# Adding seven sums of squares on VectorE, starting the turns of queries and keys earlier, and reordering the attention's first loads in a one-core layer kernel

## The chip, the core and the metric

The kernel runs on one core of a Trainium2 chip. The metric is device time in microseconds. The kernel before takes 584.43 us, the median of 3 runs (584.33 to 585.26).

## What is computed

One layer of a streaming encoder, in fp32, on 1024 tokens of width 1024 with 16 learned meta tokens in front. All three mixers read the same normalised input through one projection, and their outputs share one output projection:

```python
u = rms_norm(h, ln_w)                                # h: meta tokens + x, 1040 x 1024
cx, cb, cc, cz, cq, ckv, krope, mz, rq, rk, rv, rz = split(u @ w_in)
y_conv = cb * (causal_conv3(cc * cx) + conv_b) * silu(cz)               # width 256
q = rms_norm(rms_norm(cq) @ w_uq)                    # 8 heads of 64 + 32 rotary
k_nope, v = split(rms_norm(ckv) @ w_ukv); k = rms_norm([k_nope, krope])
y_mla = softmax(mask(rope(q) @ rope(k).T)) @ v * silu(mz)               # width 512
y_ret = retention(rope(rq), rope(rk), rv) * silu(rz)                    # width 256
out = (h + concat(y_conv, y_mla, y_ret) @ w_out)[16:]
```

The mask is causal by chunks of 64 tokens. The input norm is a factor per token, r = (mean(h*h) + eps)^-0.5, so the kernel multiplies un-normalised x with the weights and applies r afterwards.

## The kernel before

**Products in parts.** Every fp32 operand of a large product is split in a high part, a cast to the 4-byte matmul type by ScalarE, and a low part, the rest, by VectorE (`split`, L102 to L109). `mm3` (L111) then issues three matmuls, high x high, high x low and low x high, all recorded under L114. Weights come through `load_w` (L117): load, high part on ScalarE (L105), low part (L106) on VectorE, or on GpSimd where k % 3 == 2.

**Order.** The program is written in a loop order, and a scheduler orders each engine's instructions from that by its own estimate of durations. Buffers come from pools; where a tile is used again its next writer waits for the last reader. Loads go through the queue of SP, the gate weights' first ones through ScalarE's.

**Start (L190 to L235).** x^T comes in eight slices of 128 rows by 1040 columns (`xs`). Each is scaled by the norm's weight and split in four tiles: `xah`, `xal` (528 columns: meta tokens and the first 512) and `xbh`, `xbl` (the other 512). The casts are L108 on ScalarE, the low parts L109 on VectorE. ScalarE squares the slice (`xsq`, L224), and GpSimd adds the squares into `con` (L225; the first slice's squares go straight into it). The weights of the attention's gate, `wmz`, are split slice by slice. TensorE adds the slice's share to five PSUM banks of the gate `mz`, fifteen matmuls a slice.

**Norms (L242 to L255).** Nine small matmuls of `con` with ones give the sums of squares per token (`ssp`). VectorE scales them (`vx`), GpSimd takes the reciprocal root (`r`, L100), VectorE builds diagonal tiles of it (`dg`, L252), and a matmul of these with ones gives r as a row on every partition (`rps`, L254). While this runs, TensorE computes the rest of the gate. In the same stretch the up-projection weights come through one staging tile `ust` and are split (`uq`, `uk`).

**Latents, retention, convolution.** Then follow the latent projection with the attention's queries and keys, which go to memory token by token (`q_s`, `k_s`); the retention's projection and its recurrence; and the convolution in two halves of channels, each in three steps `conv_cx`, `conv_cz`, `conv_cb`. `feat` (L607) computes one projection of the convolution into one of two PSUM banks; `ccs` is the product of two of them.

**Turns (L549 to L592).** The attention wants queries and keys with features on the partitions. Eight turns, one for the keys or queries of two heads, do this in four parts: load (0), 32x32 block transposes on VectorE (1, L564), splits (2), stores to `T_s` (3). `turns()` is called once per projection step, and `slot` counts the calls: 0 to 15 in the retention, then one per convolution step, and from 36 on one per step of the attention. `BEGIN` holds the slot at which each turn starts; its parts follow 2, 3 and 4 slots later.

**Attention and output.** `load_head` brings one head's keys and queries, `load_pair` the values of two heads. `score` computes scores `S` and their exponentials on ScalarE (`pr`, L762), GpSimd normalises (L771), TensorE transposes (`pTp`, L784), ScalarE copies (`pt`, L790), and the products with the values (`o`, L825) follow. The outputs of convolution and retention (`y_s`) are multiplied with their rows of `w_out` in the gaps, token tile by token tile: `y_split` (L837) loads `ysrc` and casts it (`yh`, `yl`), `load_wo` brings the weights (`wos`), `partial` computes. The attention's own rows of `w_out` come last.

Of the kernel before, what the change touches and what calls it, by code (L numbers as in the profile page):

```python
# [7 lines left out]
F32 = mybir.dt.float32  # L8
F32R = mybir.dt.float32r
# [41 lines left out]
def trunk(tc, ins, outs):  # L51
# [121 lines left out]
    with tc.tile_pool(name="ps0", bufs=1, space=PSUM, reuse_waits="tile") as ps0:  # L173
# [18 lines left out]
        for k in range(KT):  # L192
# [27 lines left out]
            if k == 0:  # L220
                nc.scalar.activation(con[:, :L], st, AF.Square)
            else:
                sq = hp_pool.tile([P, L], F32, tag="v", name=f"xsq{k}")
                nc.scalar.activation(sq, st, AF.Square)  # L224
                nc.gpsimd.tensor_tensor(con[:, :L], con[:, :L], sq, op=ALU.add)  # L225
            if k:
# [322 lines left out]
    turned, slot = {}, [0]  # L549
    BEGIN = (3, 6, 10, 17, 21, 25, 29, 36)  # L550

    def turn(i, part):
# [14 lines left out]
        elif part == 2:  # L567
            dst = turned[i][0]
            for j in range(2):
                hi = hp_pool.tile([P, 3, 256], F32R, tag="v" if i < 6 else "k", name=f"th{i}_{j}")  # L570
                x = dst[:, 3 * j:3 * j + 3]
                if which:
                    split(hi, x.bitcast(F32R), x)
                else:

                    for c in range(3):
                        split(hi[:, c], x[:, c].bitcast(F32R), x[:, c], scale=wqk[:, c:c + 1] if c < 2 else None)
                turned[i].append(hi)
        else:
            dst, *hi = turned.pop(i)  # L580
            for j in range(2):
                nc.sync.dma_start(T_s[which][hp, 0, :, 3 * j:3 * j + 3], hi[j].bitcast(F32))
            nc.sync.dma_start(T_s[which][hp, 1], dst)
# [31 lines left out]
    def load_head(h):  # L615
        for which in (1, 0):
            for x, src in zip((qT, kT)[which][h % 2], T_s[which][h // 2]):
                src = src.rearrange("(i f) c r -> c f i r", i=4)
                o = NM * which
                for c in range(3):  # L620
                    nc.sync.dma_start(x[32 * c:32 * c + 32, o:o + SEQ].bitcast(F32).rearrange("p (i r) -> p i r", i=4), src[3 * (h % 2) + c])
        for i, m_ in enumerate((kmh, kml)):
            nc.gpsimd.tensor_copy(kT[h % 2][i][:96, :NM], m_[:, h].bitcast(F32))

# [85 lines left out]
    ps1, close_ps1 = pool("ps1", space=PSUM)  # L710
    kT = [[kp_.tile([104, LP], F32R, name=f"kt{i}{s}") for s in "hl"] for i in range(2)]
    qT = [[kp_.tile([104, SEQ], F32R, name=f"qt{i}{s}") for s in "hl"] for i in range(2)]
    msk = at1.tile([P, LP], F32, tag="pr", name="msk")
# [3 lines left out]
    for i in range(2):  # L717
        nc.vector.tensor_copy(qT[i][0][96:104], msk[96:104, :SEQ])
        nc.vector.tensor_copy(kT[i][0][96:104], msk2[96:104])
        for j in range(2):  # L720
            nc.gpsimd.memset(kT[i][j][:96, L:].bitcast(mybir.dt.uint32), 0)
        nc.gpsimd.memset(qT[i][1][96:104].bitcast(mybir.dt.uint32), 0)
        nc.gpsimd.memset(kT[i][1][96:104].bitcast(mybir.dt.uint32), 0)
    late = {}
# [13 lines left out]
    if True:  # L738
        prs, pts = {}, {}

        def score(h, t):
# [6 lines left out]
            for i in range(0, nb, 2):  # L748
                n = min(2, nb - i)
                sp = pst("s", f"S{h}_{t}_{i}").rearrange("p (b c) -> p b c", b=2)  # L750
                for j in range(n):
                    mm3(sp[:, j, :w], [q[:, ts_] for q in qT[h % 2]], [k[:, (i + j) * w:(i + j) * w + w] for k in kT[h % 2]], True, True)
                at["dve"] = nc.vector.tensor_reduce(sm[:, i // 2:i // 2 + 1], sp[:, :n, :w], axis=AX.XY, op=ALU.max, negate=True).ins  # L753
                chunks.append((sp[:, :n, :w], i * w, (i + n) * w, n))
# [82 lines left out]
        def y_split(t):  # L837
            src = wsp.tile([P, 512], F32, tag="ws", name=f"ysrc{t}")
            nc.sync.dma_start(src.rearrange("p (k q) -> p k q", k=4), y_s.rearrange("k p q -> p k q")[:, :, t * P:t * P + P])
            ysp[t] = [at1.tile([P, 4, P], F32R, tag=f"y{c}", name=f"y{c}{t}", bufs=2) for c in "hl"]  # L840
            split(ysp[t][0], ysp[t][1], src.rearrange("p (k q) -> p k q", k=4), lo_eng=nc.gpsimd)
# [15 lines left out]
    cuts = [load_wo(k, 0) for k in (0, 1, 6, 7)]  # L857
    for h in range(2):
        load_head(h)
    conv_cx(1, 1, 1)  # L860
# [5 lines left out]
    while cuts:  # L866
        cuts.pop(0)()
    y_split(0)
    conv_cb(1, 1)
# [6 lines left out]
    ym = [ymp.tile([P, SEQ], F32, name=f"ym{i}") for i in range(4)]  # L876
    for i in range(4):
        nc.sync.dma_start(ym[i], mz_s[i])
    late["at2"], close_at2 = pool("at2", LA - 2)
# [10 lines left out]
    for n in range(len(seq) + 1):  # L890
        if n + LA < len(seq):
            score(*seq[n + LA])
        if n < len(seq):
# [10 lines left out]
        if n < len(seq):  # L904
# [145 lines left out]
```

## Time and profile before

| | |
|---|---|
| Median of 3 runs | 584.43 us |
| The profiled execution's own time | 585.46 us |
| Its span, first to last instruction | 583.6 us |
| TensorE (PE) busy | 566.4 us, 97% |
| VectorE (DVE) busy | 353.6 us, 61% |
| ScalarE (ACT) busy | 255.0 us, 44% |
| GpSimd (POOL) busy | 235.4 us, 40% |
| Mean granted TensorE clock | 0.993 |

The span is taken on the core from the first to the last instruction; the execution's time is 1.86 us longer. "Busy" leaves out branches, semaphores and the issuing of loads. The granted clock is a share of full speed: 1.00 is 2.4 GHz, 0.50 is 1.2 GHz. A wait is the idle time of an engine just before an instruction, put down to the instruction that released it last. In names, `<-` stands between what an instruction writes and what it reads, and a DMA share over 1 means that more transfers were open than there are engines.

### The profile page before, as it was taken

To read this page: it belongs to the slowest core of one execution; us is meant where nothing else is said; L and a number is where in the kernel's file an instruction comes from. 1 tells how busy PE (TensorE), PEld (TensorE's weight loads), DVE (VectorE), ACT (ScalarE), POOL (GpSimd) and SP (SyncE) were. 2 spreads that over 40 slices of the span, in tenths; PEclk is the share of its full clock that TensorE was granted. 3 is DMA by queue.
4 is the path that set the end of the run, shared out by engine and by line. 5 is a ranking of instruction groups with operands and counts; after the bars stand their busy time and mean duration, and the time that the engine had idled before them with its cause. 6 is when DMAs were issued, how large, how long until landed. Compare 5 with 4: busy or idle time off the path is not lost.

```text
span 583.6 us, 9535 instructions
## 1 busy us (share of the span) xinstructions
PE 566.4 (97%) x3294; PEld 473.7 (81%) x3294; DVE 353.6 (61%) x769; ACT 255.0 (44%) x598; POOL 235.4 (40%) x327
## 2 busy tenths in 40 slices
PE   9959999999999999999999998899999999999997
PEld 5747889998888888888889877688888888887886
DVE  5974848887736661686445655856756756655032
ACT  7732455576334441543122226645545544654000
POOL 4842246867502321162321637524434534454000
PEclk9979999999999999999999999999999999999999
DMA  8535504357303641446157798937536538113086
GB/s 310 174 87 172 185 21 147 144 199 229 114 0 95 223 137 53 108 164 217 55 179 234 210 253 297 303 117 179 149 114 172 146 98 228 37 54 128 0 290 232
DMA packets 61952, 91.29 MB, mean 156 GB/s; under 512 B 5808, under 2 KB 36144, under 8 KB 61776
## 3 DMA queue, kind: packets, MB, share of 16 engines
q1 hardware_dynamic: 58304, 84.39, 47.0%
q10 hardware_dynamic: 3600, 6.29, 2.9%
q8 instruction: 26, 0.43, 0.3%
q14 instruction: 22, 0.18, 0.1%
HBM read 57.07 MB, written 33.59 MB: 155 GB/s over the span
## 4 chain that ended last, share of the span: by engine, by line
PE 84%; DVE 3%; DMA 2%; POOL 1%; ACT 1%; issue 1%; SPq 0%; DVEq 0%; ACTq 0%; POOLq 0%
PE r L114 16%; PE S L114 8%; PE out L114 8%; PE part L114 7%; PE A L114 7%; PE o L825 6%; PE cv L114 6%; PE pTp L784 5%; PE mz L114 4%; PE cz L114 3%; PE qps L114 3%; PE cb L114 3%; PE kps L114 1%; PE vps L114 1%; PE rsp L502 1%; PE rop L519 1%
## 5 line engine op out<-in xcount | busy, mean ns | idle before, releaser
L762 ACT ACTIVATE pr<-S,smx 128x144 f32<-128x144 f32 (+8 forms) x72 | 50.3, 700 | 36.4 <-DVE smx L753 25.6
L753 DVE TENSOR_REDUCE smx<-S 128x1 f32<-128x144 f32 (+8 forms) x72 | 50.7, 705 | 23.6 <-PE S L114 13.3
L770 POOL TENSOR_SCALAR pm<-pr,smx 128x16 f32<-128x16 f32 x64 | 18.4, 288 | 85.5 <-DVE smx L768 77.6
L784 PE MATMUL pTp<-ident,pr 128*128 128x128 f32 x288 | 46.0, 277 | 2.4 <-POOL pr L771 1.7
L790 ACT COPY pt<-pTp 128x512 f32<-128x512 f32 (+2 forms) x64 | 32.1, 504 | 36.7 <-PE pTp L784 36.6
L771 POOL TENSOR_SCALAR pr<-pr,smx 128x128 f32<-128x128 f32 (+3 forms) x64 | 48.0, 750 | 0.0
L784 PEld LDWEIGHTS pTp<-ident,pr 128*128 128x128 f32 x288 | 34.2, 140 | 11.4 <-issue 2.8
L476 POOL TENSOR_SCALAR kw<-qk,con 128x64 f32<-128x64 f32 (+1 forms) x36 | 16.3, 466 | 66.4 <-DVE qk L472 57.8
L825 PE MATMUL o<-pt,v 128*64 128x256 f32 (+2 forms) x448 | 38.9, 311 | 0.0
L825 PEld LDWEIGHTS o<-pt,v 128*64 128x64 f32 x448 | 27.1, 136 | 11.0 <-issue 4.0
L114 PE MATMUL r<-wh_r,xah 128*128 128x512 f32 (+1 forms) x80 | 30.4, 382 | 0.0
L114 PE MATMUL r<-wl_r,xah 128*128 128x512 f32 (+1 forms) x80 | 30.4, 380 | 0.0
L114 PE MATMUL r<-wh_r,xal 128*128 128x512 f32 (+1 forms) x80 | 29.8, 373 | 0.0
L938 DVE SCALAR_TENSOR_TENSOR ot<-out,xr 128x512 f32<-128x512 f32 (+1 forms) x17 | 11.2, 660 | 30.5 <-PE out L114 17.4
L114 PE MATMUL part<-woh,yh 128*128 128x512 f32 x64 | 29.5, 461 | 0.0
L114 PE MATMUL part<-wol,yh 128*128 128x512 f32 x64 | 25.6, 400 | 0.5 <-DVE wol L109 0.2
L114 PE MATMUL r<-wl_r,xbh 128*128 128x512 f32 x64 | 26.0, 407 | 0.0
L114 PE MATMUL r<-wh_r,xbl 128*128 128x512 f32 x64 | 25.8, 402 | 0.0
L114 PE MATMUL r<-wh_r,xbh 128*128 128x512 f32 x64 | 25.5, 398 | 0.0
L114 PE MATMUL part<-woh,yl 128*128 128x512 f32 x64 | 25.3, 396 | 0.0
L225 POOL TENSOR_TENSOR con<-con,xsq 128x1040 f32<-128x1040 f32 x7 | 19.1, 2724 | 8.1 <-ACT xsq L224 7.9
L833 DVE TENSOR_TENSOR ym<-o,ym 64x256 f32<-64x256 f32 x32 | 13.5, 422 | 14.1 <-PE o L827 13.3
(294 smaller groups left out, 1713.7 us busy)
## 6 DMA issues: line engine op xcount, KB each, us to landing
ws_r<-in_win SPq DMA_DIRECT2D x16, 256.0 KB, 2.9
ws_c<-in_win SPq DMA_DIRECT2D x16, 256.0 KB, 3.0
wos<-in_wout SPq DMA_DIRECT2D x16, 256.0 KB, 4.8
xp<-in_x SPq DMA_DIRECT2D x16, 256.0 KB, 3.3
p_s<-xp SPq DMA_DIRECT2D x16, 256.0 KB, 2.0
xr<-p_s SPq DMA_DIRECT2D x15, 256.0 KB, 4.0
out<-ot ACTq DMA_DIRECT2D x15, 256.0 KB, 4.3
xs<-in_xT SPq DMA_DIRECT2D x7, 520.0 KB, 6.0
```

Of the source, the lines that this page charges most:

```text
L114: m = nc.tensor.matmul(out, lhsT=x_, rhs=y_, start=first and i == 0, stop=last and i == 2)
L225: nc.gpsimd.tensor_tensor(con[:, :L], con[:, :L], sq, op=ALU.add)
L476: nc.gpsimd.tensor_scalar(kw[R, j], qk[R, 2 + j], con[R, kd0 + j:kd0 + j + 1], 1.0, op0=ALU.mult, op1=ALU.mult)
L753: at["dve"] = nc.vector.tensor_reduce(sm[:, i // 2:i // 2 + 1], sp[:, :n, :w], axis=AX.XY, op=ALU.max, negate=True).ins
L762: e = nc.scalar.activation(pr[:, c0:c1].rearrange("p (b c) -> p b c", b=n), sp, AF.Exp, bias=mx, accum_out=sm[:, 5 + i:6 + i])
L770: nc.gpsimd.tensor_scalar(pm[(2 * h + t // 4) % 2][:, t % 4, :NM], pr[:, nk - NM:nk], sm[:, 9:10], 1.0, op0=ALU.mult, op1=ALU.mult)
L771: nc.gpsimd.tensor_scalar(pr[:, :nk - NM], pr[:, :nk - NM], sm[:, 9:10], 1.0, op0=ALU.mult, op1=ALU.mult)
L784: tr_ = nc.tensor.transpose(out=tp[:, b * P:b * P + P], in_=pr[:, c0:c0 + P], identity=ident)
L790: nc.scalar.copy(pt[:, b0:b0 + nb, tt], src)
L825: nc.tensor.matmul(op[64 * cg:64 * cg + 64, c0:c1], lhsT=lv, rhs=src[:, i_, c_], start=b == 0, stop=False)
L833: nc.vector.tensor_tensor(ys, op[64 * cg:64 * cg + 64, :256].rearrange("p (a c q) -> p a c q", a=2, q=64), ys, op=ALU.mult)
L938: nc.vector.scalar_tensor_tensor(ot, acc[:, c0:c1], 0.5, xt, op0=ALU.mult, op1=ALU.add)
```

## The change

It has four parts. The seven adds of squares of slices 1 to 7 are issued on VectorE instead of GpSimd. Turns 3 to 7 start at slots 14, 18, 22, 26 and 30 instead of 17, 21, 25, 29 and 36, so that all eight end in the convolution; both high parts of turns 6 and 7 take the pool tag "v" that the other turns use. High and low part of a head's keys (and of its queries) become one tile, the queries being loaded with one DMA per 32 rows for both parts instead of two. And the first loads of the attention are written in another order: `y_split` is cut in a load and a cut, the load of token tile 0 comes between head 0 and head 1, and the gates `ym` of pairs 1 to 3 are loaded with their pair instead of at the start.

```diff
-                nc.gpsimd.tensor_tensor(con[:, :L], con[:, :L], sq, op=ALU.add)
+                nc.vector.tensor_tensor(con[:, :L], con[:, :L], sq, op=ALU.add)
...
-    BEGIN = (3, 6, 10, 17, 21, 25, 29, 36)
+    BEGIN = (3, 6, 10, 14, 18, 22, 26, 30)
...
-                hi = hp_pool.tile([P, 3, 256], F32R, tag="v" if i < 6 else "k", name=f"th{i}_{j}")
+                hi = hp_pool.tile([P, 3, 256], F32R, tag="v", name=f"th{i}_{j}")
...
-            for x, src in zip((qT, kT)[which][h % 2], T_s[which][h // 2]):
-                src = src.rearrange("(i f) c r -> c f i r", i=4)
-                o = NM * which
-                for c in range(3):
-                    nc.sync.dma_start(x[32 * c:32 * c + 32, o:o + SEQ].bitcast(F32).rearrange("p (i r) -> p i r", i=4), src[3 * (h % 2) + c])
+            src = T_s[which][h // 2].rearrange("s (i f) c r -> c f (s i) r", i=4)
+            x = ((qT, kT)[which][h % 2])[:, :, NM * which:NM * which + SEQ].bitcast(F32)
+            for c in range(3):
+                cs, y = slice(32 * c, 32 * c + 32), src[3 * (h % 2) + c]
+                if which:
+                    for s in range(2):
+                        nc.sync.dma_start(x[cs, s].rearrange("p (i r) -> p i r", i=4), y[:, 4 * s:4 * s + 4])
+                else:
+                    nc.sync.dma_start(x[cs].rearrange("p s (i r) -> p (s i) r", i=4), y)
...
         def y_split(t):
             src = wsp.tile([P, 512], F32, tag="ws", name=f"ysrc{t}")
             nc.sync.dma_start(src.rearrange("p (k q) -> p k q", k=4), y_s.rearrange("k p q -> p k q")[:, :, t * P:t * P + P])
+            return lambda: y_cut(t, src)
+
+        def y_cut(t, src):
             ysp[t] = [at1.tile([P, 4, P], F32R, tag=f"y{c}", name=f"y{c}{t}", bufs=2) for c in "hl"]
...
-    for h in range(2):
-        load_head(h)
+    load_head(0)
+    y0 = y_split(0)
+    load_head(1)
...
-    y_split(0)
+    y0()
...
-    for i in range(4):
-        nc.sync.dma_start(ym[i], mz_s[i])
+    nc.sync.dma_start(ym[0], mz_s[0])
...
                 pairs.append(load_pair(h // 2 + 1))
+                nc.sync.dma_start(ym[h // 2 + 1], mz_s[h // 2 + 1])
```

The order of VectorE's instructions in the start stage, from the low parts of slice 5 on, as a difference (+ is new; the number after a name is the slice, then the tile's own number):

```order
 L109 SCALAR_TENSOR_TENSOR xal5_311<-xs5_308,vec_78,xah5_310 128x528
 L109 SCALAR_TENSOR_TENSOR xbl5_315<-xs5_308,vec_78,xbh5_314 128x512
+L225 TENSOR_TENSOR con_107<-con_107,xsq5_318 128x1040
 L109 SCALAR_TENSOR_TENSOR xal6_345<-xs6_342,vec_78,xah6_344 128x528
 L109 SCALAR_TENSOR_TENSOR xbl6_349<-xs6_342,vec_78,xbh6_348 128x512
 L109 SCALAR_TENSOR_TENSOR xal7_379<-xs7_376,vec_78,xah7_378 128x528
 L109 SCALAR_TENSOR_TENSOR xbl7_383<-xs7_376,vec_78,xbh7_382 128x512
+L225 TENSOR_TENSOR con_107<-con_107,xsq6_352 128x1040
 L106 TENSOR_TENSOR wl_mz6_358<-ws_mz6_355,wh_mz6_357 128x512
 L106 TENSOR_TENSOR wl_mz7_392<-ws_mz7_389,wh_mz7_391 128x512
+L225 TENSOR_TENSOR con_107<-con_107,xsq7_386 128x1040
+L109 SCALAR_TENSOR_TENSOR uq1_616<-ust0_619,vec_78,uq0_615 128x768
```

Each add stands behind low parts of x, that of slice 5 right in front of the next low parts, the add of slice 6 in front of the low parts of weights 6 and 7, and the add of slice 7 in front of the first split of an up-projection weight. On GpSimd the two low parts of weights 2 and 5 stay and the seven adds go.

The order on VectorE at the start of the convolution, where `cv` is a PSUM bank, `qk` belongs to the last retention step and `td3` is a tile of turn 3. Before:

```order
L641 TENSOR_TENSOR ccs0_2781<-cv0_1_14_2782,rb_112 128x258
L493 SCALAR_TENSOR_TENSOR zsb1_4_2582<-zsb1_4_2582,rt1_7_2762 128x128
L472 TENSOR_TENSOR qk1_7_2764<-qk1_7_2764 128x256
L106 TENSOR_TENSOR wl_c13_2994<-ws_c13_2991,wh_c13_2993 128x512
L641 TENSOR_TENSOR ccs0_2781<-cv0_1_272_2817,rb_112 128x256
L514 SCALAR_TENSOR_TENSOR state1_1551<-state1_1551,con_107,rup1_5_2699 64x64 x2
L644 TENSOR_TENSOR ccs0_2781<-cv0_0_14_2861,ccs0_2781 128x258
L564 STREAM_TRANSPOSE td3_2919<-ts3_2854 128x8x3x32 x2
```

Now:

```order
L646 TENSOR_TENSOR ccs0_2786<-cv0_1_14_2787,rb_112 128x258
L493 SCALAR_TENSOR_TENSOR zsb1_4_2582<-zsb1_4_2582,rt1_7_2767 128x128
L472 TENSOR_TENSOR qk1_7_2769<-qk1_7_2769 128x256
L564 STREAM_TRANSPOSE td3_2820<-ts3_2725 128x8x3x32 x2
L106 TENSOR_TENSOR wl_c13_3005<-ws_c13_3002,wh_c13_3004 128x512
L109 SCALAR_TENSOR_TENSOR td3_2820<-td3_2820,wqk_94,th3_0_2862 128x256
L646 TENSOR_TENSOR ccs0_2786<-cv0_1_272_2825,rb_112 128x256
```

The two transposes of turn 3 and one of its low parts have moved from behind the third evacuation of a convolution bank (L644) to ahead of the second (L641, now L646).

The order on ScalarE at the start of the attention, where `pr0_t` are the exponentials of head 0 and token tile t, `yh` the casts of the convolution and retention outputs, and `pt` copies of transposed scores. Before:

```order
L762 ACTIVATE pr0_0_3542,smx0_0_3536<-S0_0_0_3537,smx0_0_3536 128x144
L663 ACTIVATE th1_1_3549<-z1_1_3548 128x512
L762 ACTIVATE pr0_1_3589,smx0_1_3583<-S0_1_0_3584,smx0_1_3583 128x272
L105 CAST yh0_3615<-ysrc0_3613 128x512
L762 ACTIVATE pr0_2_3600,smx0_2_3594<-S0_2_0_3595,smx0_2_3594 128x400
L790 COPY pt0_0_3727<-pTp0_0_0_3728 128x128
L790 COPY pt0_0_3727<-pTp0_1_0_3767 128x2x128
L762 ACTIVATE pr0_3_3708,smx0_3_3699<-S0_3_0_3700,smx0_3_3699 128x528
L105 CAST yh1_3742<-ysrc1_3740 128x512
```

Now:

```order
L105 CAST yh0_3630<-ysrc0_3467 128x512
L660 ACTIVATE yv1_1_3561<-ccs1_3206,vec_78 128x512
L767 ACTIVATE pr0_0_3556,smx0_0_3550<-S0_0_0_3551,smx0_0_3550 128x144
L668 ACTIVATE th1_1_3563<-z1_1_3562 128x512
L767 ACTIVATE pr0_1_3606,smx0_1_3600<-S0_1_0_3601,smx0_1_3600 128x272
L767 ACTIVATE pr0_2_3617,smx0_2_3611<-S0_2_0_3612,smx0_2_3611 128x400
L105 CAST yh1_3750<-ysrc1_3748 128x512
L795 COPY pt0_0_3739<-pTp0_0_0_3740 128x128
L795 COPY pt0_0_3739<-pTp0_1_0_3775 128x2x128
L767 ACTIVATE pr0_3_3720,smx0_3_3711<-S0_3_0_3712,smx0_3_3711 128x528
```

The cast of token tile 0 (`yh0`) has moved from behind the second exponential to ahead of the first, and that of token tile 1 (`yh1`) from behind the fourth exponential to ahead of it and of the first copies.

## Rows read from the trace of the kernel before

**Rows 1.** The profile's first part: each engine's busy us, share of the span, instructions.

```profile
PE 566.4 (97%) x3294; PEld 473.7 (81%) x3294; DVE 353.6 (61%) x769; ACT 255.0 (44%) x598; POOL 235.4 (40%) x327
```

**Rows 2.** Waits of TensorE, whole span: who waited for whom, us, times, longest.

```profile
PE mz L114 <- DVE wl_mz L106: 6.0, 1, 6.0
PE S L114 <- ACT pr L762: 1.9, 1, 1.9
PE pTp L784 <- POOL pr L771: 1.7, 1, 1.7
```

**Rows 3.** Windows: stretch; PE, PEld, DVE, ACT, POOL busy; PEclk, DMA, GB/s.

```profile
25.00:31.00 6.00, 6.00 (x27) 4.85 (x26) 6.00 (x4) 5.29 (x9) 5.92 (x4) 1.00 0.29 97
...
37.50:43.00 5.50, 5.50 (x13) 4.33 (x14) 3.20 (x5) 1.66 (x4) 1.07 (x1) 0.50 0.74 217
```

**Rows 4.** VectorE to 45 us, by shape: busy us, mean ns, idle before.

```profile
L109 DVE SCALAR_TENSOR_TENSOR xal<-xs,vec,xah 128x528 fp32r<-128x528 f32 x7 | 15.1, 2164 | 1.3 <-ACT xah L108 1.3
L109 DVE SCALAR_TENSOR_TENSOR xbl<-xs,vec,xbh 128x512 fp32r<-128x512 f32 x7 | 11.6, 1656 | 0.0
L106 DVE TENSOR_TENSOR wl_mz<-ws_mz,wh_mz 128x512 fp32r<-128x512 f32 x6 | 4.0, 682 | 0.6 <-ACT wh_mz L105 0.6
```

**Rows 5.** VectorE in order of time: start us, us, instruction.

```profile
14.73 2.95 DVE L109 SCALAR_TENSOR_TENSOR xal<-xs,vec,xah 128x528 fp32r<-128x528 f32 x1
...
21.04 0.76 DVE L109 SCALAR_TENSOR_TENSOR xal<-xs,vec,xah 128x528 fp32r<-128x528 f32 x1
...
38.40 1.01 DVE L109 SCALAR_TENSOR_TENSOR uq<-ust,vec,uq 128x768 fp32r<-128x768 f32 x1
...
51.66 1.28 DVE L252 TENSOR_TENSOR dg<-ident,r 128x512 f32<-128x512 f32 x2
```

**Rows 6.** GpSimd in order of time, 10 to 26 us.

```profile
10.08 2.45 POOL L225 TENSOR_TENSOR con<-con,xsq 128x1040 f32<-128x1040 f32 x1 [5.12 <-ACT xsq L224]
...
14.22 5.75 POOL L225 TENSOR_TENSOR con<-con,xsq 128x1040 f32<-128x1040 f32 x2
22.75 2.62 POOL L225 TENSOR_TENSOR con<-con,xsq 128x1040 f32<-128x1040 f32 x1 [2.78 <-ACT xsq L224]
```

**Rows 7.** GpSimd, 8 to 45 us, groups by shape.

```profile
L225 POOL TENSOR_TENSOR con<-con,xsq 128x1040 f32<-128x1040 f32 x7 | 19.1, 2724 | 8.1 <-ACT xsq L224 7.9
L106 POOL TENSOR_TENSOR wl_mz<-ws_mz,wh_mz 128x512 fp32r<-128x512 f32 x2 | 3.5, 1765 | 0.0
```

**Rows 8.** VectorE, 45 to 64 us, groups by shape.

```profile
L106 DVE TENSOR_TENSOR wl_A<-ws_A,wh_A 128x416 fp32r<-128x416 f32 x3 | 1.8, 587 | 1.1 <-ACT wh_A L105 0.7 <-PE mz L114 0.4
```

**Rows 9.** TensorE in order of time, 30 to 57 us.

```profile
30.77 0.40 PE L114 MATMUL mz<-xah,wh_mz 128*128 128x512 f32 x1
31.00 0.39 PE L114 MATMUL mz<-xal,wh_mz 128*128 128x512 f32 x1
37.42 0.79 PE L114 MATMUL mz<-xah,wl_mz 128*128 128x512 f32 x1 [6.03 <-DVE wl_mz L106]
...
43.11 0.39 PE L114 MATMUL mz<-xah,wh_mz 128*128 128x512 f32 x1
...
46.58 1.97 PE L242 MATMUL ssp<-ones,con 128*128 128x1 f32 x18
...
56.27 1.88 PE L254 MATMUL rps<-dg,ones 128*128 128x512 f32 x4
```

**Rows 10.** VectorE in order of time, the start of the convolution.

```profile
261.79 0.41 DVE L641 TENSOR_TENSOR ccs<-cv,rb 128x256 f32<-128x256 f32 x1
...
264.60 1.83 DVE L564 STREAM_TRANSPOSE td<-ts 128x768 f32<-128x768 f32 x2
```

**Rows 11.** TensorE in order of time, the start of the convolution.

```profile
263.99 0.28 PE L114 MATMUL cv<-xah,wh_c 128*128 128x256 f32 x1
```

**Rows 12.** ScalarE in order of time, the start of the attention.

```profile
352.84 0.62 ACT L105 CAST yh<-ysrc 128x512 fp32r<-128x512 f32 x1 [6.32 <-DMA ysrc<-y_s]
```

**Rows 13.** Windows, 3 us of the attention's start.

```profile
342.00:345.00 3.00, 2.80 (x15) 2.22 (x14) 0.77 (x3) 0.47 (x2) 1.07 (x3) 1.00 1.12 224
```

More of the change, by code (lines that the diff above doesn't have):

```diff
@@ L616, in load_head @@
         for which in (1, 0):
-            for x, src in zip((qT, kT)[which][h % 2], T_s[which][h // 2]):
-                src = src.rearrange("(i f) c r -> c f i r", i=4)
-                o = NM * which
-                for c in range(3):
-                    nc.sync.dma_start(x[32 * c:32 * c + 32, o:o + SEQ].bitcast(F32).rearrange("p (i r) -> p i r", i=4), src[3 * (h % 2) + c])
+            src = T_s[which][h // 2].rearrange("s (i f) c r -> c f (s i) r", i=4)
[7 more added lines that the diff above has]
+                    nc.sync.dma_start(x[cs].rearrange("p s (i r) -> p (s i) r", i=4), y)
         for i, m_ in enumerate((kmh, kml)):
-            nc.gpsimd.tensor_copy(kT[h % 2][i][:96, :NM], m_[:, h].bitcast(F32))
+            nc.gpsimd.tensor_copy(kT[h % 2][:96, i, :NM], m_[:, h].bitcast(F32))
     def load_pair(hp):
@@ L710, in trunk @@
     ps1, close_ps1 = pool("ps1", space=PSUM)
-    kT = [[kp_.tile([104, LP], F32R, name=f"kt{i}{s}") for s in "hl"] for i in range(2)]
-    qT = [[kp_.tile([104, SEQ], F32R, name=f"qt{i}{s}") for s in "hl"] for i in range(2)]
+    kT = [kp_.tile([104, 2, LP], F32R, name=f"kt{i}") for i in range(2)]
+    qT = [kp_.tile([104, 2, SEQ], F32R, name=f"qt{i}") for i in range(2)]
     msk = at1.tile([P, LP], F32, tag="pr", name="msk")
@@ L717, in trunk @@
     for i in range(2):
-        nc.vector.tensor_copy(qT[i][0][96:104], msk[96:104, :SEQ])
-        nc.vector.tensor_copy(kT[i][0][96:104], msk2[96:104])
+        nc.vector.tensor_copy(qT[i][96:104, 0], msk[96:104, :SEQ])
+        nc.vector.tensor_copy(kT[i][96:104, 0], msk2[96:104])
         for j in range(2):
-            nc.gpsimd.memset(kT[i][j][:96, L:].bitcast(mybir.dt.uint32), 0)
-        nc.gpsimd.memset(qT[i][1][96:104].bitcast(mybir.dt.uint32), 0)
-        nc.gpsimd.memset(kT[i][1][96:104].bitcast(mybir.dt.uint32), 0)
+            nc.gpsimd.memset(kT[i][:96, j, L:].bitcast(mybir.dt.uint32), 0)
+        nc.gpsimd.memset(qT[i][96:104, 1].bitcast(mybir.dt.uint32), 0)
+        nc.gpsimd.memset(kT[i][96:104, 1].bitcast(mybir.dt.uint32), 0)
     late = {}
@@ L751, in score @@
                 for j in range(n):
-                    mm3(sp[:, j, :w], [q[:, ts_] for q in qT[h % 2]], [k[:, (i + j) * w:(i + j) * w + w] for k in kT[h % 2]], True, True)
+                    mm3(sp[:, j, :w], [qT[h % 2][:, s, ts_] for s in range(2)], [kT[h % 2][:, s, (i + j) * w:(i + j) * w + w] for s in range(2)], True, True)
                 at["dve"] = nc.vector.tensor_reduce(sm[:, i // 2:i // 2 + 1], sp[:, :n, :w], axis=AX.XY, op=ALU.max, negate=True).ins
@@ L917, in trunk @@
                     if m % 8 == 0 and m // 8 + 1 < NT:
-                        y_split(m // 8 + 1)
+                        y_split(m // 8 + 1)()
                     with tc.issue_after(late["pe"]):
```

## The prediction

> **What bounds the kernel now.** I read the busy shares first, then the waits of TensorE, then the table by stage, then the instructions around each wait. TensorE is busy 97% of the span [rows 1], so an edit can pay only where TensorE stands still or runs slowly. The list of its waits is short [rows 2]: 6.0 us on the low part of a gate weight, split by VectorE; 1.9 us on an exponential of ScalarE and 1.7 us on a normalised score row of GpSimd, both at the start of the attention. The first is the largest and has a tail: in the 5.5 us after it the granted clock is 0.50, the lower of the two levels (1.2 GHz); before the idle stretch it was 1.00 [rows 3].
>
> Who is late at 31 us? VectorE is busy for all 6.00 us from 25 to 31 [rows 3]. The low parts xal and xbl take 2.16 and 1.66 us in the mean, and the low part of a weight 0.68 us [rows 4]. Singly they show two prices: 2.95 us at 14.73, 0.76 us at 21.04 [rows 5]. GpSimd tells which is which: its adds of squares begin at 10.08, two of them run from 14.22 to 19.97, and the next starts at 22.75 [rows 6]; the long instructions stand beside them, the short one in its pause. In the 5.75 us of those two adds VectorE gets through two instructions.
>
> **Part 1: seven sums of squares go to VectorE.** Removed: seven GpSimd adds at 2.72 us [rows 7], and with them the stretch of VectorE's low parts. Against 0.76 and 0.74 us undisturbed (the 0.76 of rows 5; xbl has 0.02 us less for 16 fewer elements), seven xal give back 7 x (2.16 - 0.76) = 9.8 us, seven xbl 7 x (1.66 - 0.74) = 6.4 us, together 16.2 us. Two GpSimd instructions stay, the low parts of weights 2 and 5, at 1.77 us each [rows 7]; they may keep 3.5 us of the 16.2. Added on VectorE: seven adds of 128x1040, which no row shows. The nearest is the same kind of instruction at 512 elements, 0.68 us [rows 4], and at 416, 0.59 us [rows 8]: 1 ns an element, so 0.68 + 528 x 0.001 = 1.2 us, 8.4 us for seven. Ends: 0.68 us (no price for length) and 2.72 us (GpSimd's own price for this add).
>
> VectorE so gains 16.2 - 3.5 - 8.4 = 4.3 us at least. But the adds stand in its order before the splits that TensorE needs, so I followed the order forward. From the first add, at 10.1 us as now, to the low part of weight 7 there are twelve low parts of x at 0.75, four of weights at 0.68, six adds at 1.2 and two GpSimd blocks of 1.77 us: 9.0 + 2.7 + 7.2 + 3.5 = 22.4 us, so 32.5 us at the latest (the rows overlap a little), and weight 6 at 31.8. TensorE now: the wait runs from 31.23 (the start at 31.00 and one matmul; these start every 0.23 us, as at 30.77 and 31.00) to 37.42, 6.2 us, and behind it thirteen matmuls from 37.42 to 43.11 take 5.7 us instead of 3.0 [rows 9]. Without both, 6.2 + 2.7 = 8.9 us, the matmul of the sums that starts at 46.58 starts at 37.7. Counted back from there, fifteen matmuls to a slice of x, slice 7 begins at 34.2 and wants its low weight as the third, at 34.6; slice 6 begins at 30.7 and wants it as the eleventh, at 33.0. So TensorE doesn't wait, by 1 to 2 us, and the part is worth the whole 8.9 us. With 2.72 us an add, VectorE ends 9 us later, TensorE waits 7.8 us in place of 6.2, and the part costs 1.6 us. At 0.68 us nothing more is won, as TensorE is already full.
>
> The Trainium skill (SBUF — State Buffer, Who interferes with whom) says that a VectorE instruction with two SBUF inputs and a GpSimd instruction that reads SBUF exclude each other for the whole instruction, whoever comes first. The trace agrees: two VectorE instructions in the 5.75 us of two GpSimd adds. The rule also speaks against the edit, since the new adds have two SBUF inputs and can hold off the two splits left on GpSimd; by that the split of weight 5 comes up to 1.2 us later, TensorE still has it in time, and the sum stays. The same skill (VectorE: DVE Perf Modes, The TRN2 errata — SBUF-src ops pay a fixed extra latency per instruction) gives a fp32 add as (N + 151)/0.96 ns, 1.24 us here, an estimate of 8.7 us for seven; the sum by it is the same.
>
> What is late next: the reciprocal norms. Two up-projection weights are staged through one tile, and VectorE computes the norms behind the last of these splits. The chain starts with the split of 38.40, and the diagonal tiles that end it are ready at 51.66 + 1.28 = 52.9 [rows 5], 14.5 us later; TensorE wants them at 56.27 [rows 9]. The split now comes behind the last add, at 32.5 to 33.7, so the chain ends at 47.0 to 48.2, while TensorE wants it at 56.27 - 8.9 = 47.4. I take a loss of 0.3 us (0 to 1.5).
>
> **Part 2: all turns end in the convolution.** Turns 3 to 7 start at slots 14, 18, 22, 26 and 30. At the start of the convolution the two transposes of turn 3, 1.83 us, and a low part of 256 columns (by rows 8, 0.59 less 0.16, some 0.4 us) now stand before the product that frees the second convolution bank. That product started at 261.79 and took 0.41 us [rows 10]; with 2.2 us more it ends at 264.4. The matmuls that need the bank began at 263.99 [rows 11], so TensorE waits about 0.5 us (0 to 1.5: one more low part and the transposes' half). Later turns lie beside steps of 24 matmuls or 5.6 us, in each of which VectorE has one evacuation. Turn 7 leaves the attention, where its transposes, of the same price, and its casts stood on the engines behind the 1.7 us wait.
>
> **Part 3: the first loads.** The loads of head 0 shrink from twelve issues to nine, and the convolution output of token tile 0 is fetched before head 1 instead of behind it. ScalarE stood 6.32 us before that cast, until 352.84 [rows 12], and everything behind it was late: this is the 1.9 us wait. It goes. But the second such cast has moved ahead of the copies of the first transposes and of the fourth exponential in ScalarE's order, and its load still sits behind head 1 and four weight tiles in a stretch where the 16 DMA engines are full (share 1.12 at 342 to 345 us [rows 13]) with the same bytes; I charge 0.5 us for it. From the 1.7 us wait I credit 0.6 us. Sum 1.9 + 0.6 - 0.5 = 2.0 us; ends 0 and 3.6 us (all of 1.9 and 1.7). The gate loads of pairs 1 to 3 move later, each beside a head's worth of matmuls: nothing.
>
> **Sum.** 8.9 - 0.3 - 0.5 + 2.0 = 10.1 us. The profiled execution took 585.46 us, 1.03 above the median of 584.43; 585.46 - 10.1 = 575.4, on the median's level 574.3 us, which is the forecast.
>
> **Rivals.**
> 1. VectorE still ends last in the start stage: the add costs more than 1.2 us, or the two GpSimd splits block longer. For it: the margin is 1 to 2 us on 21 us of work. Against: rows 4 and 8 give this instruction one price per element. At 1.9 us an add VectorE ends 4.2 us later, TensorE waits some 3 us and 2 us of the slow clock return: 8.9 shrinks to 4, and with 1.5 us for the rest the time is 578.9 us.
> 2. The attention start pays in full and nothing else is late: 584.43 - (8.9 + 3.6) = 571.9 us. For it: ScalarE is no longer held. Against: DMA engines are full there.
> 3. The chain of norms and the convolution's start take their upper ends, 1.5 us each: 584.43 - (8.9 - 3.0 + 2.0) = 576.5 us. For it: both have lost their slack. Against: the chain's loads have fewer others beside them.
> 4. Slower: GpSimd is not what stretches VectorE; the instructions merely coincide, and writing or loading the same x tiles stretches them. Then 8.4 us of adds stand on the engine that ends last, the wait grows from 6.2 to 14.6 us, and with 1.5 us from the attention the time is 584.43 + 8.4 - 1.5 = 591.3 us. It decides from the point where under 8.4 of the 16.2 us vanish. Against: the 0.76 us in GpSimd's pause.
>
> **How the numbers follow.** Forecast (572.5 to 576) 0.53; rival 1 0.12; rival 2 and below 0.14; rival 3 0.15; rival 4 0.04; 0.02 for no change. By the SBUF page's rule all overlap with the removed adds must vanish, which is why rival 4 has no more. A change below 0.2% (1.2 us) can't be told here. Faster 0.94, same 0.02, slower 0.04. The range 570.0 to 578.5 us takes in rivals 2 and 3 and the near half of rival 1.
>
> **What would show it.** Part 1: xal and xbl near 0.75 us, the adds near 1.2 us, no TensorE wait between 20 and 40 us, clock 1.00 there, the sums matmul near 37.7 us, its diagonal matmul about 9 us earlier than before. Part 2: a wait for the second product at the convolution's start; no transposes after 350 us on that clock. Part 3: the first cast of the convolution output done before the third exponential; no wait of the fifth score tile. Wrong would be: a TensorE wait over 2 us before 40 us, a VectorE add over 1.6 us, or attention waits that add up to more than before.

## The result and the profile after

The changed kernel takes 578.03 us (median of 4 runs, 576.35 to 579.68) against 584.5 us, a ratio of 0.9887 with a 95% interval of 0.9854 to 0.9919: 6.5 us faster, where 10.1 were forecast. A second set of six runs gave 0.9881 (0.9849 to 0.9912). The profiled execution took 579.68 us, the slowest of the first four, with a span of 577.8 us.

The start stage came out as forecast. The first part of the page of after, and below it the same windows as in [rows 3], with the one between them (columns as there):

```profile
PE 566.9 (98%) x3294; PEld 475.1 (82%) x3294; DVE 355.0 (61%) x776; ACT 253.5 (44%) x598; POOL 219.2 (38%) x320
```

```profile
25.00:31.00 6.00, 6.00 (x27) 4.88 (x27) 6.00 (x9) 2.65 (x4) 0.00 (x0) 1.00 0.15 38
31.00:37.50 6.50, 6.50 (x29) 5.22 (x29) 3.49 (x6) 2.97 (x5) 1.08 (x1) 1.00 0.57 190
37.50:43.00 5.50, 5.50 (x35) 4.80 (x34) 1.52 (x6) 0.72 (x1) 1.50 (x1) 1.00 0.61 181
```

TensorE has no gap and its clock stays at 1.00. The groups of VectorE by shape up to 45 us of after answer to [rows 4]:

```profile
L225 DVE TENSOR_TENSOR con<-con,xsq 128x1040 f32<-128x1040 f32 x7 | 8.6, 1230 | 0.1
L109 DVE SCALAR_TENSOR_TENSOR xal<-xs,vec,xah 128x528 fp32r<-128x528 f32 x7 | 7.4, 1055 | 0.0
L109 DVE SCALAR_TENSOR_TENSOR xbl<-xs,vec,xbh 128x512 fp32r<-128x512 f32 x7 | 5.2, 739 | 0.0
L106 DVE TENSOR_TENSOR wl_mz<-ws_mz,wh_mz 128x512 fp32r<-128x512 f32 x6 | 4.0, 681 | 0.7 <-ACT wh_mz L105 0.7
```

The adds took 1.23 us each (1.2 forecast); xal and xbl together fell from 26.7 to 12.6 us, by 14.1 us (forecast: 16.2, of which the two GpSimd splits might keep 3.5). In after, TensorE's matmul of the sums and that of the diagonal tiles, which stood at 46.58 and 56.27 [rows 9], are these:

```profile
38.27 1.97 PE L242 MATMUL ssp<-ones,con 128*128 128x1 f32 x18
...
47.97 1.02 PE L254 MATMUL rps<-dg,ones 128*128 128x512 f32 x2
```

Both are 8.3 us earlier. The latent matmuls behind them show the whole of it. From the view of the latent projection's tile, of before and then of after (ns least/median/most, first and last start):

```profile
L114 PE MATMUL A<-wh_A,xah x40: 233/350/455, 63.8 to 89.8; 128*128 128x416 f32 x32, 128*16 128x160 f32 x8
```

```profile
L114 PE MATMUL A<-wh_A,xah x40: 233/351/457, 54.8 to 80.8; 128*128 128x416 f32 x32, 128*16 128x160 f32 x8
```

The start is worth 63.8 - 54.8 = 9.0 us, by these two executions. It is known to about 1 us: in the traces of the runs below the same matmuls start at 53.9 to 54.8 us with the adds on VectorE (pool_copy, which adds work there, apart), and at 62.6 us with them on GpSimd (adds_back). What is lost is lost later. The waits of TensorE in after, whole span, against [rows 2]:

```profile
PE pTp L789 <- ACT pt L795: 2.8, 2, 2.6
...
PE cv L114 <- DVE ccs L646: 0.5, 2, 0.3
PE part L114 <- DVE wol L109: 0.5, 1, 0.5
PE S L114 <- ACT pr L767: 0.3, 1, 0.3
PE pTp L789 <- POOL pr L776: 0.3, 1, 0.3
```

The 6.0, 1.9 and 1.7 us of before are gone; the 0.3 us on `pr` by ScalarE and by GpSimd come at other places (364.11 and 343.02 us). The first row is new but for 0.2 us. ScalarE in order of time, after:

```profile
334.59 0.62 ACT L105 CAST yh<-ysrc 128x512 fp32r<-128x512 f32 x1 [8.38 <-DMA ysrc<-y_s]
...
348.14 0.62 ACT L105 CAST yh<-ysrc 128x512 fp32r<-128x512 f32 x1 [6.06 <-DMA ysrc<-y_s]
348.67 0.53 ACT L795 COPY pt<-pTp 128x128 f32<-128x128 f32 x2
```

The cast of token tile 0 no longer holds an exponential. (It still holds `yv`, the convolution's last activation, whose input VectorE had ready at 330.9 us and which begins at 335.12; TensorE doesn't wait for that.) The cast of token tile 1, which before began at 356.45 us without a wait, now waits 6.06 us for its load, and the first copies of transposes stand behind it on ScalarE. Its load, on SP's queue in after, is the last of these:

```profile
333.02 2.32 SPq L626 DMA_DIRECT2D qt<-qT_s  x3
...
336.22 0.34 SPq L583 DMA_DIRECT2D qT_s<-td  x1
336.85 2.92 SPq L693 DMA_DIRECT2D wos<-in_wout  x4
340.92 0.38 SPq L844 DMA_DIRECT2D ysrc<-y_s  x1
```

It is issued at 340.92, behind head 1, the stores of turn 7 and four weight tiles, and the cast begins at 348.14, 7.2 us later. TensorE meanwhile, and then windows of after, one of 2 us and three of 10:

```profile
346.05 0.39 PE L114 MATMUL part<-woh,yl 128*128 128x512 f32 x1
349.07 0.87 PE L789 MATMUL pTp<-ident,pr 128*128 128x128 f32 x3 [2.63 <-ACT pt L795]
```

```profile
350.00:352.00 2.00, 2.00 (x7) 1.71 (x7) 0.94 (x3) 1.57 (x4) 1.93 (x5) 0.51 1.01 334
340.00:350.00 10.00, 7.05 (x36) 5.74 (x36) 3.62 (x8) 3.10 (x11) 5.36 (x9) 0.93 1.07 370
350.00:360.00 10.00, 10.00 (x65) 8.34 (x65) 6.64 (x16) 5.74 (x13) 7.72 (x13) 0.90 0.90 311
360.00:370.00 10.00, 9.07 (x48) 7.49 (x47) 6.36 (x16) 6.35 (x17) 4.79 (x9) 0.83 1.02 220
```

Behind the gap of 2.63 us the clock falls to half, as it did at 37.5 us before [rows 3]. Over the three longer stretches it lacks 0.7 + 1.0 + 1.7 = 3.4 us of full speed; the last 1.7 belong to a second drop after 365 us. That one came behind two short gaps, 0.35 us on an exponential and 0.5 us on `wol`; the trace of after_again has the same two gaps and no second drop, so it doesn't come with the program every time.

### The profile page after: what moved, and what is told of

Its sections match the earlier page's. It is cut to its first block, busy times and chain, and to the rows that moved or that the text cites. A ratio compares the mean times of both kernels' runs of the same rounds, so it can differ in the third digit from the quotient of the medians.

```text
span 577.8 us, 9510 instructions
## 1 busy us (share of the span) xinstructions
PE 566.9 (98%) x3294; PEld 475.1 (82%) x3294; DVE 355.0 (61%) x776; ACT 253.5 (44%) x598; POOL 219.2 (38%) x320
## 4 chain that ended last, share of the span: by engine, by line
PE 80%; DMA 10%; DVE 4%; POOL 2%; ACT 1%; issue 1%; SPq 1%; DVEq 0%; ACTq 0%; POOLq 0%
PE r L114 15%; PE S L114 9%; PE mz L114 8%; PE part L114 7%; PE A L114 7%; PE o L830 6%; PE pTp L789 5%; DMA out<-ot 4%; PE cv L114 3%; PE out L114 3%; PE qps L114 3%; DMA ysrc<-y_s 3%; PE cz L114 2%; PE cb L114 2%; DMA ts<-q_s 1%; PE kps L114 1%
## 5 line engine op out<-in xcount | busy, mean ns | idle before, releaser
L114 PE MATMUL S<-kt,qt 104*128 104x144 f32 (+6 forms) x336 | 66.4, 331 | 0.4 <-ACT pr L767 0.3
L114 PEld LDWEIGHTS S<-kt,qt 104*128 104x128 f32 x336 | 56.0, 193 | 7.0 <-ACT pr L767 1.5
L789 PEld LDWEIGHTS pTp<-ident,pr 128*128 128x128 f32 x288 | 35.1, 143 | 12.5 <-issue 6.4
L476 POOL TENSOR_SCALAR kw<-qk,con 128x64 f32<-128x64 f32 (+1 forms) x36 | 16.2, 464 | 67.4 <-DVE qk L472 57.2
```

The lines of the kernel that those rows point to most:

```text
L114: m = nc.tensor.matmul(out, lhsT=x_, rhs=y_, start=first and i == 0, stop=last and i == 2)
L476: nc.gpsimd.tensor_scalar(kw[R, j], qk[R, 2 + j], con[R, kd0 + j:kd0 + j + 1], 1.0, op0=ALU.mult, op1=ALU.mult)
L789: tr_ = nc.tensor.transpose(out=tp[:, b * P:b * P + P], in_=pr[:, c0:c0 + P], identity=ident)
```

## The experiments

The theory after this: the start pays its 9 us; the turns and the loads pay too; the cast of token tile 1 takes back more than they pay. The rival: an attention that begins earlier meets its loads earlier and gives 2 to 3 us back whatever their order is. Ratios are to the kernel before as it was timed together with each run, with 95% intervals. It took 585.2 to 585.8 us there instead of 584.5, so the ratios compare and the medians alone don't.

| run | edit | median us | ratio |
|---|---|---|---|
| adds_only | before, adds on VectorE | 577.74 | 0.9855 (0.9835 to 0.9876) |
| adds_back | after, adds on GpSimd | 586.10 | 1.0014 (0.9992 to 1.0036) |
| y1_late_cut | after, casts of tiles 1 to 7 later | 573.50 | 0.9789 (0.9769 to 0.9810) |
| late_cut_again | the same | 574.20 | 0.9799 (0.9771 to 0.9826) |
| y1_early | after, load of tile 1 earlier | 574.89 | 0.9810 (0.9789 to 0.9830) |
| fix_turns_back | y1_late_cut, old turns | 576.69 | 0.9849 (0.9823 to 0.9876) |
| adds_turns | before, adds and new turns | 575.76 | 0.9824 (0.9794 to 0.9854) |
| adds_y0 | adds_only, casts later | 577.76 | 0.9875 (0.9846 to 0.9905) |
| after_again | the changed kernel | 578.13 | 0.9881 (0.9849 to 0.9912) |

**The adds alone, and all but the adds.** adds_only is the kernel before with this edit, adds_back the changed kernel with its reverse:

```diff
-                nc.gpsimd.tensor_tensor(con[:, :L], con[:, :L], sq, op=ALU.add)
+                nc.vector.tensor_tensor(con[:, :L], con[:, :L], sq, op=ALU.add)
```

> The kernel before, with only the seven adds of squares moved to VectorE; later turns and first loads as before. Theory A (the adds are the whole gain; in the changed kernel the first latent matmul stands 9.0 us earlier than before, and the attention then gives part of it back because the cast of token tile 1 holds ScalarE): nothing gives back here, so 584.5 - 9.0 = 575.5 us, between 575.0 and 576.5, faster than the changed kernel, and TensorE's waits of 1.9 and 1.7 us at the attention's start stay as before. Theory B (the adds gain only about 6.5 us by the end, since a kernel that starts its attention earlier meets its loads earlier and gives 2 to 3 us back whatever the order of the first loads is): 577.5 to 578.5 us, with attention waits longer than before.

> The changed kernel with the seven adds back on GpSimd; turns and first loads stay changed. Theory A (turns and loads together cost time, since the cast of token tile 1 stands ahead of the first copies on ScalarE): 584.5 + 0.5 to 2.5 us, 585 to 587 us, with a TensorE wait of over 1.5 us on a copy of a transpose at the attention's start. Theory B (turns and loads pay the 1.5 us of the forecast, and it is the adds that paid less): 582.5 to 583.5 us.

adds_only gives 0.0145 x 584.5 = 8.5 us, 576.0 us on the recorded level and within theory A's range; its median of 577.74 us would have been theory B's, but the kernel before was slower beside it as well, 585.56 us. That the adds alone gain more than the whole change (8.5 against 6.5 us) is not clear by these two ratios, whose intervals overlap; adds_back says it from the other side. The waits of adds_only:

```profile
PE pTp L784 <- POOL pr L771: 1.7, 1, 1.7
PE S L114 <- ACT pr L762: 1.5, 1, 1.5
...
PE S L114 <- DMA qt0h<-qT_s: 1.0, 1, 1.0
```

The old waits of the attention stay, and the first score's wait for its queries grows from 0.6 to 1.0 us. That is the part of theory B that can be seen: in the kernels with the adds on VectorE the first score waits 0 to 1.8 us for a load. adds_back, 1.0014 (0.9992 to 1.0036), shows that turns and loads together pay nothing while the cast stands where it stands; the two largest of its waits:

```profile
PE mz L114 <- DVE wl_mz L106: 6.0, 1, 6.0
PE pTp L789 <- ACT pt L795: 3.4, 2, 3.3
```

**The cast of token tile 1.** y1_late_cut issues the cast behind the exponential issued last, on ScalarE (with its low part on GpSimd), and leaves the load. Its expectation speaks of one instruction, but the edit stands in a loop and moves the casts of token tiles 1 to 7. y1_early moves one load, that of tile 1, and leaves every cast's place in the program:

```diff
-                        y_split(m // 8 + 1)()
+                        yc = y_split(m // 8 + 1)
+                        with tc.issue_after(late["act"]):
+                            yc()
```

```diff
     y0 = y_split(0)
+    y1 = y_split(1)
...
-                        y_split(m // 8 + 1)()
+                        (y1 if m == 0 else y_split(m // 8 + 1))()
```

> The changed kernel with one instruction moved: ScalarE's cast of token tile 1 is issued behind the exponentials of token tile 4 instead of ahead of the first copies; its load and everything else stay. Theory A (the wait of 2.6 us and the stretch at half clock behind it come from this cast alone): both go; 2.6 us and some 1.3 us of clock less than the profiled 579.7 us, so 574.5 to 576 us, and the mean clock is 1.00 in all runs. Theory B (the copies are late for another reason: the transfers of the attention's start are full, or scores come late): 577 to 579 us, another wait of about 2 us in its place.

> The changed kernel with the load of token tile 1 issued right behind that of token tile 0, ahead of head 1, so that it lands before ScalarE comes to the cast. Theory A: the wait of 2.6 us and its stretch at half clock go, as in the kernel that moves the cast; 574.5 to 576 us, the cast waits for no load. Theory B (transfers, not the order on ScalarE, decide: 0.25 MB that come earlier push head 1 and the weights of the output back by about 1 us, and a later matmul waits for these): 577 to 579 us.

> The changed kernel once more, beside the next run on one chip, for the price of the cast of token tile 1 from runs taken together: 0.986 to 0.990 of the kernel before, with the 2.6 us wait on a copy at the attention's start.

> The changed kernel with the late cast once more: 0.977 to 0.981 of the kernel before, 4 to 6 us faster than the changed kernel of the same call. If the cast were worth only its wait of 2.6 us and no clock, 2 to 3 us.

after_again and late_cut_again were timed together: the casts' place costs 578.13 - 574.20 = 3.9 us by the medians and 0.0082 x 584.5 = 4.8 us by the ratios, more than the wait, which is 2.76 us in the trace of after_again. y1_late_cut came out below theory A's range. That it is the cast of tile 1 and not the six later ones follows from y1_early, which moves nothing but the load of tile 1 and gains 0.0071 x 584.5 = 4.1 us on after_again, though not timed together with it. ScalarE of y1_late_cut around the cast, and its windows:

```profile
342.28 0.27 ACT L795 COPY pt<-pTp 128x128 f32<-128x128 f32 x1 [0.64 <-PE pTp L789]
...
347.11 0.62 ACT L105 CAST yh<-ysrc 128x512 fp32r<-128x512 f32 x1 [0.86 <-DMA ysrc<-y_s]
```

```profile
340.00:350.00 10.00, 9.66 (x55) 8.35 (x55) 5.57 (x12) 4.99 (x14) 8.74 (x14) 1.00 1.08 375
350.00:360.00 10.00, 9.57 (x68) 7.08 (x67) 6.87 (x20) 7.41 (x20) 5.21 (x9) 1.00 0.94 312
360.00:370.00 10.00, 9.49 (x77) 7.43 (x77) 6.45 (x16) 3.95 (x12) 5.95 (x12) 1.00 0.89 174
```

From issue to landing the load takes as long as in after (340.04 to 347.11, 7.1 us), the copies no longer care, and the clock holds. The spread of the changed kernel's runs goes with the clock: those with a mean clock of 1.000 took 576.35, 577.26 and 577.95 us, those with 0.994 took 579.68, 580.14 and 581.46, the other four 576.71 to 578.81; with the late casts all stand at 0.999 or 1.000, at 572.5 to 574.9 us. So the wait costs some 3 us where the clock holds and about twice that where it falls furthest. y1_early cures the wait too: the cast waits 0.69 us for its load and begins at 337.60, ahead of the first exponential. A score waits 1.3 us in its trace, put down to the load that was moved ahead of head 1; but that first score waits 1.3 us on a load in late_cut_again and 1.8 us in fix_turns_back too, where that load was not moved, so theory B's price isn't shown by it.

**Turns and loads apart.** fix_turns_back is y1_late_cut, adds_turns is adds_only, with the table and the tag exchanged:

```diff
-    BEGIN = (3, 6, 10, 14, 18, 22, 26, 30)
+    BEGIN = (3, 6, 10, 17, 21, 25, 29, 36)
```

```diff
-    BEGIN = (3, 6, 10, 17, 21, 25, 29, 36)
+    BEGIN = (3, 6, 10, 14, 18, 22, 26, 30)
```

> The changed kernel with the late cast of token tile 1, and with the turns at their old slots, so that turn 7's transposes and casts lie in the attention again. It prices the turns alone, against 0.979 of the kernel before that the same kernel with the new slots reached. Theory A (the turns were the cause of the 1.7 us wait on a normalised score row, and cost 0.5 us at the convolution's start): that wait comes back with a stretch at half clock, the convolution's wait goes; 1 to 3 us slower, 0.981 to 0.984 of the kernel before. Theory B (the turns pay nothing, what was won there is the loads' doing): 0.978 to 0.980.

> The kernel before with the adds on VectorE and the new slots of the turns; head tiles and first loads as before. It prices the loads. So far, as shares of the kernel before: adds alone 0.9855, adds and loads with the late cast but old turns 0.985, all with the late cast 0.979. Theory A (turn 7 in the attention was the cause of the 1.7 us wait and of the half clock behind it, so the turns pay about 3.5 us by themselves, and the loads little): 0.979 to 0.982. Theory B (turns and loads pay only together: without the new loads the attention's start keeps a wait on a cast or on a load of 1.5 us or more with its stretch at half clock): 0.983 to 0.986.

With the old turns 2.9 to 3.5 us are lost, 0.0050 x 584.5 against late_cut_again and 0.0060 x 584.5 against y1_late_cut, neither timed together with fix_turns_back: somewhat more than theory A's range. Its other half failed, for the wait at the convolution's start did not go (1.0 us on `ccs`). Without the new loads the turns are worth 0.0031 x 584.5 = 1.8 us (adds_turns against adds_only), with intervals that overlap. A wait and a window of fix_turns_back, and a wait of adds_turns:

```profile
361.94 0.65 PE L789 MATMUL pTp<-ident,pr 128*128 128x128 f32 x4 [1.69 <-POOL pr L776]
```

```profile
360.00:370.00 10.00, 8.31 (x44) 5.60 (x44) 7.88 (x21) 6.09 (x18) 4.57 (x10) 0.83 1.11 261
```

```profile
346.11 0.42 PE L114 MATMUL S<-kt0h,qt0h 104*128 104x328 f32 x1 [1.63 <-ACT pr L762]
```

With turn 7 back in the attention, the 1.7 us wait on GpSimd is back and with it a drop of the clock of 0.17 x 10 = 1.7 us, together 3.4 us, about what is lost. (A wait of 1.8 us on a load of keys is in that trace too, one of 1.3 us in that of late_cut_again and none in that of y1_late_cut: it comes and goes.) In adds_turns that wait is gone and the one on the held exponential stays: the turns cure the one, the loads the other. By its time adds_turns lies between the two theories, and its interval takes in most of both.

**The order without the loads.** adds_y0 is adds_only with the casts later in ScalarE's order:

```diff
-            split(ysp[t][0], ysp[t][1], src.rearrange("p (k q) -> p k q", k=4), lo_eng=nc.gpsimd)
+            with tc.issue_after(late["act"]):
+                split(ysp[t][0], ysp[t][1], src.rearrange("p (k q) -> p k q", k=4), lo_eng=nc.gpsimd)
```

> The kernel before with the seven adds on VectorE and with one more edit: the casts of token tiles are written behind the exponentials that were issued last, so that the first of them comes behind the third exponential; turns and loads as before. Theory A (at the attention's start a cast that waits for its load holds what stands behind it on ScalarE, and the order alone is the price): TensorE's 1.5 us wait on an exponential goes without any load moved, and 1 to 2 us of 577.7 go: 0.982 to 0.984 of the kernel before. Theory B (the loads' time is the price: the cast, later in the order, holds the first copies of transposes instead): 0.985 to 0.988, with a wait of 1.5 us or more on a copy in its place.

It gains nothing. The wait on the exponential goes, and others take its place, if not the one that theory B named:

```profile
PE pTp L784 <- POOL pr L771: 1.7, 1, 1.7
...
PE o L827 <- DMA vr<-v_s: 1.1, 1, 1.1
PE part L114 <- POOL yl L106: 0.6, 1, 0.6
```

So moving the cast of token tile 0 alone was not enough, where for token tile 1 either edit was. No run moves the load of tile 0 alone, so what its new place pays by itself is not shown; loads and late casts together give 1.5 to 2.0 us (0.9799 and 0.9789 against adds_turns, with intervals that overlap).

**What stretched VectorE.** Two kernels, made from y1_late_cut with one GpSimd instruction of 128x1040 beside each add, ran once each: 579.69 us with the copies, where the norms come late and TensorE waits 2.8 us for `rb`, and 574.09 us with the fills, against 572.60 to 574.89 us of y1_late_cut:

```diff
                 nc.vector.tensor_tensor(con[:, :L], con[:, :L], sq, op=ALU.add)
+                nc.gpsimd.tensor_copy(rb, sq)        # pool_copy
+                nc.gpsimd.memset(sq, 0.0)            # pool_memset, instead
```

> The changed kernel with the late cast, with seven extra copies of the squares on GpSimd (into a tile that is not used yet), so that GpSimd reads 128x1040 of SBUF beside VectorE's low parts while the sums stay on VectorE. Theory A (a VectorE instruction with two SBUF inputs and a GpSimd instruction that reads SBUF hold each other off): VectorE's low parts beside a copy stretch by up to the copy's own time again, the mean of xal and xbl rises from 1.06 and 0.74 us to 1.2 us or more. Rival 4 of the forecast (the stretch came from loading or writing the x slices and coincided with the adds): they stay at 1.06 and 0.74 us.

> The same place, but GpSimd only writes: seven fills of the tile of squares behind the adds, 128x1040 each, no input. Theory A (it is GpSimd's reading that collides): xal and xbl keep 1.06 and 0.74 us in the mean and the adds 1.23 us, though the fills lie beside them. The rival that any GpSimd instruction of this size stretches VectorE: 1.2 us or more, as with the copies.

VectorE's groups in pool_copy and then in pool_memset, and behind each one GpSimd instruction of it:

```profile
L225 DVE TENSOR_TENSOR con<-con,xsq 128x1040 f32<-128x1040 f32 x7 | 9.5, 1354 | 0.2
L109 DVE SCALAR_TENSOR_TENSOR xbl<-xs,vec,xbh 128x512 fp32r<-128x512 f32 x7 | 7.8, 1115 | 0.0
L109 DVE SCALAR_TENSOR_TENSOR xal<-xs,vec,xah 128x528 fp32r<-128x528 f32 x7 | 6.9, 985 | 0.1
L106 DVE TENSOR_TENSOR wl_mz<-ws_mz,wh_mz 128x512 fp32r<-128x512 f32 x6 | 5.2, 865 | 0.7 <-ACT wh_mz L105 0.7
```

```profile
25.01 1.42 POOL L226 COPY rb<-xsq 128x1040 f32<-128x1040 f32 x1 [2.06 <-ACT xsq L224]
```

```profile
L225 DVE TENSOR_TENSOR con<-con,xsq 128x1040 f32<-128x1040 f32 x7 | 8.6, 1230 | 0.1
L109 DVE SCALAR_TENSOR_TENSOR xal<-xs,vec,xah 128x528 fp32r<-128x528 f32 x7 | 7.4, 1056 | 0.1
L109 DVE SCALAR_TENSOR_TENSOR xbl<-xs,vec,xbh 128x512 fp32r<-128x512 f32 x7 | 5.2, 740 | 0.0
L106 DVE TENSOR_TENSOR wl_mz<-ws_mz,wh_mz 128x512 fp32r<-128x512 f32 x6 | 4.0, 682 | 0.6 <-ACT wh_mz L105 0.6
```

```profile
14.95 0.97 POOL L226 MEMSET xsq<- 128x1040 f32 x1 [1.53 <-DVE con L225]
```

The copies lengthen these four groups from 25.2 to 29.4 us (five of the seven stand beside them), the fills by nothing. The sizes that theory A expected were too high: xbl rose to 1.12 us only, and xal fell to 0.99, because in y1_late_cut it was xal that stood beside the two GpSimd splits and here it was others. But reading it is: a copy of the squares touches no slice of x, and VectorE stretches beside it, so the forecast's fourth rival falls.

## Why the prediction was right, and where it missed

The direction, the place and the mechanism of the main term were right, and the time lies in the range, 3.7 us above the forecast. That it lies inside is in part luck: it is 0.5 us from the upper end, four of the ten executions took more than 578.5 us, and that end had been set by rivals 1 and 3, neither of which came. Of the forecast's signs of being wrong the last is undecided: the attention's waits add up to 4.2 us in after and 5.3 us in after_again, against 5.1 us before.

- **Part 1** (8.9 us forecast): 9.0 at the first latent matmul, 8.5 us (7.2 to 9.6) for adds_only as a whole kernel. Rival 1, that VectorE still ends last, did not come: its last gate weight was done at 29.6 us, not 32.5. Each GpSimd split cost VectorE 1.0 us (an xal of 1.80 instead of 0.76), not 1.77, and rows that overlap make up most of the rest. The 1.77 us probably hold waiting of GpSimd's own: in pool_copy a split of this shape took 1.29 us.
- **The chain of norms** (0.3 forecast as a loss): nothing. The first up-projection split began at 30.72 us and the diagonal tiles were ready at 44.7, 3.3 us ahead of their matmul.
- **Part 2, the convolution's start** (0.5 us as a loss): too small to tell. The forecast's wait, for the second product, came and took 0.23 us (the second line, of after). The other 0.31 us are a wait for the first product, which the kernel before has too, 0.93 us long (the first line); the forecast overlooked it. From the first latent matmul to the first `cz` matmul, TensorE takes 203.5 to 204.3 us in the traces of after and of the six runs of the table with the new slots, and 203.5 to 204.2 in the four traces with the old, so no loss shows.

```profile
260.32 0.39 PE L114 MATMUL cv<-xah,wh_c 128*128 128x258 f32 x1 [0.93 <-DVE ccs L641]
```

```profile
255.23 0.39 PE L114 MATMUL cv<-xah,wh_c 128*128 128x256 f32 x1 [0.23 <-DVE ccs L646]
```

- **The turns in the attention** (0.6 us credited from the 1.7): mis-sized. They are worth 2.9 to 3.5 us with the new loads, the wait and as much again in clock, and 1.8 us without them. In the profiled execution of the kernel before this wait had no drop of the clock behind it, so no row could give that half. It may have been an exception: of the 17 executions of that kernel timed with adds_only, 12 had a mean clock below its 0.993, down to 0.988, but no trace of these was kept.
- **Part 3, the term that was wrong:** "I charge 0.5 us" for the second cast ahead of the copies and the fourth exponential. It was the right place at an eighth to a tenth of its price: a wait of 2.63 us and, in six of ten runs, a mean clock of 0.996 or less, together 3.9 to 4.8 us. The rows to size it were there: the first cast had waited 6.32 us for a load in the same stretch of full queues [rows 12, 13], and nothing in the change moved the second load ahead of head 1 or the weights. The forecast worked its 0.5 us out from no row; what had to be priced was the distance between ScalarE's reaching the cast (342.09) and the load's landing (348.14), less the work that TensorE still had.

With the casts put behind, adds, turns and loads together reach 0.979 and 0.980, which are 11.7 to 12.3 us, close to the second rival's 12.5. y1_late_cut is the fastest version that was run.

## What to carry to other kernels

Where an instruction that waits for a load moves ahead in an engine's order, price it from the load's own landing time, not from how much the queue changed; all that stands behind it waits as long. Where TensorE is 97% busy, price a wait once as idle time and once more as a chance of lost clock: of the four waits of 1.68 or 1.69 us in these traces, three were followed by a drop that lost another 1.7 us. And where VectorE ends last, look at what GpSimd reads from SBUF beside it: here an add cost VectorE 1.23 us of its own, and on GpSimd, at 2.72 us, it lengthened VectorE's low parts by 14.1 / 7 = 2.0 us.

## What the runs showed of the hardware

- GpSimd's fills (0.97 us, write only) ran beside VectorE's two-input instructions and stretched none of them; its copies, which read, took 1.05 to 2.13 us and stretched VectorE by 4.2 us in all. The Trainium skill (SBUF — State Buffer, Who interferes with whom) says that such VectorE instructions contend with a GpSimd instruction that reads SBUF and not with one that only writes; these two traces agree.
- The same wait of 1.68 us was followed by no drop of the clock in the kernel before, and by a stretch at half clock in adds_only (in adds_y0 and, behind 1.69 us, in fix_turns_back as well). Windows right behind it, of before and of adds_only:

```profile
372.00:374.00 2.00, 1.82 (x11) 1.47 (x12) 2.00 (x6) 2.00 (x7) 0.12 (x1) 1.00 0.93 282
```

```profile
363.00:365.00 2.00, 1.90 (x8) 1.72 (x9) 2.00 (x6) 2.00 (x7) 0.04 (x1) 0.50 0.54 140
```

What decides between them is left open: in adds_only the wait came 9.1 us earlier in the span, with the same program around it. It differs between executions of one kernel too: four of fix_turns_back have a mean clock of 0.996 or 0.997, the fifth 0.999.
